# Layer 1's gates and memory queries by seven products of halves, in a stage ahead of its heads

## The chip, the core and the metric

The kernel runs on one core of a Trainium2 chip. The core has five engines, each with an instruction queue of its own that is worked off in order: TensorE (PE in the profile; its weight loads are PEld), VectorE (DVE), ScalarE (ACT), GpSimd (POOL), and SyncE (SP), which here only issues DMAs. They wait for one another through semaphores. Matmul operands lie in SBUF (128 partitions), matmul results in PSUM, which has eight banks of 128 x 512 fp32.

The metric is the device time of one execution in microseconds. Three runs of the kernel before gave 1555.32, 1557.88 and 1558.98 us, median 1557.88.

## The reference

A two-layer encoder over 1024 tokens of width 1024. Each layer normalises its input, makes one large input projection that feeds several groups of attention heads and a gate, multiplies the heads' outputs by silu of the gate, and projects back with a residual. Layer 0 has global heads, window heads and four memory heads; layer 1, which the change is about, has 16 heads of neighbourhood attention (C) and four memory heads:

```python
h = rmsnorm(x, norm_gain[l])
...
qc, kc, vc, qm, gate = split_cols(h @ w_in_odd[o], SPLIT_ODD)
yc = neighborhood_attn(qc.reshape(B, S, C_HEADS, HEAD_DIM),
                       kc.reshape(B, S, C_HEADS, HEAD_DIM),
                       vc.reshape(B, S, C_HEADS, HEAD_DIM), rpb_c[o])
ym = memory_attn(qm.reshape(B, S, M_HEADS, M_HEAD_DIM), mk, mv)
y = jnp.concatenate([yc, ym], axis=-1) * jax.nn.silu(gate)
x = x + y @ w_out_odd[o]
```

In layer 1, `qc`, `kc` and `vc` have 1024 columns each, `qm` 512 and `gate` 1536.

## The kernel before

Tokens lie along the free dimension (columns) and features along the partitions, so a normalised input is eight tiles of 128 features x 1024 tokens. All matmuls are fp32r, and a product keeps fp32 precision by three of them: every operand is split into a high part (a copy rounded to fp32r, made by ACT or POOL) and a low part (the difference, made by DVE or POOL), and high x high, high x low and low x high are summed in PSUM. The normalised input is held as tiles `H`, eight high ones and eight low ones. In the code `self.split`, `self.w_parts` and `self.wparts` are such splits; a weight block is loaded as `wraw`, and its parts are `wh` and `wl`, of four buffers each.

A projection of 128 columns (`tokens`, `token_steps`) takes two halves of 512 tokens, each 8 feature tiles x 3 matmuls of 128x512: 48 matmuls in a bank `pj`. A sink (`q_pair`, `k_pair`, `gate`, `mem_q`) then takes the result out of PSUM.

A scheduler puts the instructions of each engine in an order before the run; the program's own order is the start, `self.ahead(kind)` moves a group ahead or back by a number of the table `AHEAD`, `issue_after` ties a group behind one instruction, and `keep_in_program_order` pins one. Work can be put off: `put_off` and `lazily` collect generators in `self.waiting`, and `pull(n)` issues the next n steps of them.

The program's stages are: preparation, layer 0's heads (phase `l0`), its output projection (`out_project`), layer 1 (phase `l1`, function `odd`), and its output projection.

`out_project` already works by seven products: the weights and the gated outputs are cut into halves, sums of halves of the weights are made beforehand by POOL (`weight_sums`), and of the outputs when they are gated. It ends with the second half of the tokens (columns 512 to 1023): for each of its eight tiles the residual is added, `square` makes a square on ACT (tile `bt`, one buffer) and POOL adds the squares up (`vt`); the last addition, on DVE, gives the row sums of squares `rows1`. The first half's statistics come earlier, and that half is normalised completely (`norm_split`). For the second half, `each` puts the tokens times the gain, without their norm, into `H` (`with_gain`), and layer 1 multiplies by the norm later: `with_rstd` multiplies a sink's input by the norm along the columns (DVE, tile `vt`) where the column is from `raw_from` on, and `values` and `mem_att` use the norms as a scale per row.

Layer 1 begins with the first two memory queries, and after the first half of the first one `stats` computes the norms: four small matmuls (`rstd_cols`), eleven small DVE operations for the reciprocal root (`rq_v`, `rq_i`, `rq_y`, `rq_t`), and four transposes that turn them into rows (`rows_of`). Then come four memory heads (`mem_att`), with the values' projections (`values`), the other memory queries and a gate for each head issued between them in whole, and eight pairs of neighbourhood heads (`near_head`). A neighbourhood head has eight blocks of 128 queries: scores (two matmuls, tile `s`), bias and maximum (DVE, tile `pn`), exponential (ACT), reciprocal (DVE), normalisation (POOL), transposes on PE (`tr`), high and low parts (`ph` by ACT, `pl` by DVE), and the products with the values (`pv`). Behind each pair stand its gate (48 matmuls), `gated_rows` and the next pair's keys and queries (96 matmuls); the scheduler spreads them over the heads. The last pair has other cover: two gates put off and the begin of the output projection.

## Time and profile before

| what | us |
|---|---|
| median of three runs | 1557.88 |
| the profiled execution, its own time | 1557.26 |
| its span, first to last instruction | 1555.4 |
| busy in the span: PE, DVE, ACT, POOL | 1507.2, 993.5, 789.2, 742.8 |
| output projection of layer 0 ends, layer 1's projections begin | at 812 |
| layer 1's memory heads | about 842 to 1040 |
| layer 1's neighbourhood heads | about 1045 to 1414 |

The profile is that of one execution. Its page gives busy time and shares for each engine and the chain of work that ended last; the answers of the trace used below list groups of instructions (line of the code, engine, operation, output<-inputs, shapes, count, busy time in us, mean in ns, and the engine's idle time ahead of them with what ended it), waits, stretches, and single instructions in order of time. A matmul's listed duration runs from its own start, while its predecessor may still be draining, so durations of matmuls overlap.

### The profile page before, as it was taken

To read this page: it belongs to the slowest core of one execution; us is meant where nothing else is said; L and a number is where in the kernel's file an instruction comes from. 1 tells how busy PE (TensorE), PEld (TensorE's weight loads), DVE (VectorE), ACT (ScalarE), POOL (GpSimd) and SP (SyncE) were. 2 spreads that over 40 slices of the span, in tenths; PEclk is the share of its full clock that TensorE was granted. 3 is DMA by queue.
4 is the path that set the end of the run, shared out by engine and by line. 5 is a ranking of instruction groups with operands and counts; after the bars stand their busy time and mean duration, and the time that the engine had idled before them with its cause. 6 is when DMAs were issued, how large, how long until landed. Compare 5 with 4: busy or idle time off the path is not lost.

```text
span 1555.4 us, 24589 instructions
## 1 busy us (share of the span) xinstructions
PE 1507.2 (97%) x8166; PEld 1290.7 (83%) x8166; DVE 993.5 (64%) x2162; ACT 789.2 (51%) x1798; POOL 742.8 (48%) x859
## 2 busy tenths in 40 slices
PE   6999999999999999999999999999999999989997
PEld 5899898888888788778877878888888888878786
DVE  7768677767676668777483242346666666676654
ACT  8644556656655355655352232335554555565443
POOL 2513455546474545533464151246554666654454
PEclk7999999999999999999999999999999999999998
DMA  9535333132231513278545243444354554657844
GB/s 350 184 98 160 96 101 117 62 137 89 82 126 51 169 39 109 95 237 296 174 143 163 82 135 109 151 117 129 128 159 130 168 176 148 189 164 263 287 124 134
DMA packets 156670, 228.32 MB, mean 147 GB/s; under 512 B 13184, under 2 KB 95360, under 8 KB 155520
## 3 DMA queue, kind: packets, MB, share of 16 engines
q1 hardware_dynamic: 155680, 226.02, 44.9%
q8 instruction: 64, 1.05, 0.3%
q10 hardware_dynamic: 864, 0.74, 0.2%
q14 instruction: 62, 0.51, 0.1%
HBM read 152.26 MB, written 65.01 MB: 140 GB/s over the span
## 4 chain that ended last, share of the span: by engine, by line
PE 83%; DMA 5%; DVE 5%; ACT 3%; POOL 2%; issue 2%; SPq 0%; DVEq 0%; ACTq 0%; POOLq 0%
PE pj L212 34%; PE tr L107 9%; PE pj L363 6%; PE pv L907 4%; PE sa L1102 3%; PE pj L1102 3%; PE pv L944 3%; PE pj L704 3%; PE tr L1102 2%; PE sa L874 2%; PE sa L875 2%; PE s L1102 2%; PE pj L145 1%; DMA wraw<-w_o 1%; PE s L961 1%
## 5 line engine op out<-in xcount | busy, mean ns | idle before, releaser
L212 PE MATMUL pj<-H,wh 128*128 128x512 f32 x1696 | 559.4, 405 | 1.3 <-DVE q L301 0.7
L212 PEld LDWEIGHTS pj<-H,wh 128*128 128x128 f32 x1696 | 304.9, 189 | 53.2 <-DVE q L301 1.0
L212 PE MATMUL pj<-H,wl 128*128 128x512 f32 x848 | 336.5, 397 | 0.0
L99 ACT ACTIVATE ph<-tr 128x512 fp32r<-128x512 f32 (+2 forms) x336 | 178.9, 540 | 182.8 <-PE tr L107 179.2
L428 DVE TENSOR_TENSOR pl<-tr,ph 128x512 fp32r<-128x512 f32 (+2 forms) x336 | 204.6, 615 | 62.8 <-ACT ph L99 60.3
L212 PEld LDWEIGHTS pj<-H,wl 128*128 128x128 f32 x848 | 160.0, 189 | 34.6
L129 POOL TENSOR_SCALAR wh<-wraw 128x512 fp32r<-128x512 f32 x114 | 74.2, 651 | 192.3 <-PE pj L212 163.4
L130 POOL TENSOR_TENSOR wl<-wraw,wh 128x512 fp32r<-128x512 f32 x114 | 153.9, 1352 | 23.5 <-ACT wh L99 13.4
L107 PE MATMUL tr<-ident,P 128*128 128x128 f32 x816 | 127.4, 275 | 2.5 <-POOL P L585 2.0
L1056 POOL TENSOR_TENSOR wl<-wraw,wh 128x384 fp32r<-128x384 f32 x56 | 63.2, 1130 | 111.1 <-ACT wh L99 93.2
L975 POOL TENSOR_SCALAR pn<-pn,st 128x384 f32<-128x384 f32 (+1 forms) x128 | 75.6, 594 | 79.8 <-DVE st L974 66.6
L99 ACT ACTIVATE wh<-wraw 128x384 fp32r<-128x384 f32 (+1 forms) x138 | 73.4, 540 | 76.3 <-PE tr L1102 14.7
L107 PEld LDWEIGHTS tr<-ident,P 128*128 128x128 f32 x816 | 97.7, 141 | 12.8 <-POOL P L585 3.0
L882 POOL TENSOR_SCALAR P<-P,st 128x1024 f32<-128x1024 f32 x64 | 75.5, 1182 | 67.0 <-DVE st L881 61.2
L973 ACT ACTIVATE pn<-pn,st 128x384 f32<-128x384 f32 (+1 forms) x128 | 74.7, 585 | 40.7 <-DVE st L972 36.8
L880 ACT ACTIVATE P<-sa,st 128x1024 f32<-128x1024 f32 x64 | 71.5, 1118 | 41.6 <-DVE st L879 22.3
L518 POOL TENSOR_SCALAR P<-P,st 128x256 f32<-128x256 f32 x64 | 31.6, 510 | 124.9 <-DVE st L516 124.8
L879 DVE TENSOR_REDUCE st<-sa 128x1 f32<-128x1024 f32 x64 | 77.6, 1218 | 13.0 <-PE sa L875 12.0
L363 PE MATMUL pj<-k,H 128*128 128x512 f32 x256 | 81.4, 390 | 0.0
L969 DVE CUSTOM_DVE_ANT_0 pn<-s,bm 128x384 f32<-128x384 f32 x96 | 52.5, 555 | 35.6 <-PE s L962 15.6
L704 PE MATMUL pj<-ah,H 128*128 128x256 f32 x384 | 73.3, 287 | 0.0
L585 POOL TENSOR_SCALAR P<-P,st 128x384 f32<-128x384 f32 (+1 forms) x64 | 39.1, 628 | 59.3 <-DVE st L580 51.7
(416 smaller groups left out, 3586.3 us busy)
## 6 DMA issues: line engine op xcount, KB each, us to landing
wraw<-w_o SPq DMA_DIRECT2D x80, 256.0 KB, 3.0
y<-sg SPq DMA_DIRECT2D x24, 512.0 KB, 2.9
y<-yb SPq DMA_DIRECT2D x24, 512.0 KB, 3.1
wraw<-s SPq DMA_DIRECT2D x64, 192.0 KB, 3.6
wraw<-w_e SPq DMA_DIRECT2D x44, 256.0 KB, 3.0
k<-k SPq DMA_DIRECT2D x36, 256.0 KB, 4.5
wraw<-w_mem SPq DMA_DIRECT2D x32, 256.0 KB, 4.4
v<-ph SPq DMA_DIRECT2D x32, 256.0 KB, 2.1
```

Of the source, the lines that this page charges most:

```text
L99: return self.nc.scalar.activation(out, in_, AF.Copy, scale=scale)
L107: self.turned = self.fence = self.nc.tensor.transpose(o, i, self.ident)
L130: (nc.gpsimd if self.wsplit[1] == "pool" else nc.vector).tensor_tensor(lf, raw, hf, op=OP.subtract)
L212: last = nc.tensor.matmul(a[:, :n], s[:, kt % UNIT, :], m, start=(kt == 0 and i == 0), stop=(kt == KT - 1 and i == 2))
L363: nc.tensor.matmul(p, x[kt][:, t], m, start=(kt + i == 0), stop=(kt == KT - 1 and i == 2))
L428: nc.vector.tensor_tensor(pl[:, :n], tr[:, :n], ph[:, :n], op=OP.subtract)
L704: self.last = nc.tensor.matmul(a[:, b * 256:(b + 1) * 256], x[kt][:, t], w, start=(kt + b + i == 0), stop=(kt == KT - 1 and i == 2), skip_ ...
L879: nc.vector.tensor_reduce(st[:, 0:1], s, axis=AX.X, op=OP.max, negate=True)
L882: self.normal = nc.gpsimd.tensor_scalar(pt, pt, st[:, 2:3], 0.5, op0=OP.mult, op1=OP.mult)
L973: nc.scalar.activation(o, o, AF.Exp, bias=st[:, 1:2], accum_out=st[:, 2:3])
L975: normal = nc.gpsimd.tensor_scalar(o, o, st[:, 3:4], 0.5, op0=OP.mult, op1=OP.mult)
L1102: last = nc.tensor.matmul(bank, s[:, k, :], y[3 * u + k][m][:, cols], start=start and u + k + e == 0, stop=u == 1 and k + e == 4, skip_gro ...
```

## The change

A new stage, `front`, stands between layer 0's output projection and layer 1's heads. It computes ten of layer 1's twelve gates (8 to 11 and 0 to 5) and its four memory queries, in seven pairs of projections. With the weights of a pair cut into quarters (two column blocks by two halves of the features) and the tokens into quarters (two halves of the features by two halves of the tokens), a pair is a product of 2x2 by 2x2 blocks, and it is made by seven block products in place of eight. A block product is 12 matmuls of 128x512.

The seven products need sums and differences of the quarters. On the weights' side they are four operations of 128x512 for each pair (`sums`, on POOL; on DVE for the second pair). On the tokens' side they are made once (`operands`): the second half is now normalised completely, in `x1`, the fp32 tiles that the output projection left (tags `P` and `yb`, in a pool `mid` that lives on into the stage); from it and the first half the differences t1 to t4 are made and split into parts. The differences of t1 and t2 are DVE's, those of t3 and t4 POOL's; all low parts of t1 to t4 are DVE's. `each`, `with_gain`'s use for the second half, and the multiplication by the norm in layer 1's sinks fall away (`raw` takes the place of `raw_from`, and only layer 0 has it).

While these operands are made, PE works on the two products of the first five pairs that need only the first half of the tokens (`begin` and `second`, 24 matmuls a pair): 24 of those ahead of the statistics, 12 between them and the turn into rows, and 60 behind the turn, ahead of the first product with t1; the remaining 24 stand between the first pair's products with t1 and t2. `begin` uses five banks `x`, `second` the one bank `pv`, which DVE must have read before it is used again.

Results go to DRAM: a gate as gate x (1 + tanh) (512 tokens a store), a memory query as high and low parts. Layer 1 loads them with one DMA a tile.

In layer 1 the values' projections are put off and pulled in steps of 12 matmuls at the memory heads, and the keys and queries of the next pair are put off and pulled in steps of 3 matmuls, two steps a block. The copies of a key's halves to the other partitions move into its sink.

In the diff, the first part is the new stage:

```diff
+    def front(self, w, pairs, early, order, x1, squares, dests):
...
+        def operands():
+            with self.ahead("norm"):
+                y = self.rstd_cols([squares], 1, 4)
+            yield self.last
+            with self.ahead("norm"):
+                rows = self.rows_of(y, 4)
...
+                for n in range(len(todo) + 2):
+                    if n < len(todo):
+                        x, kt, _, _ = todo[n]
+                        d = nc.vector.scalar_tensor_tensor(x, x, self.gain[:, 8 + kt:9 + kt], rows, op0=OP.mult,
+                                                           op1=OP.mult)
+                        if n:
+                            pin(d)
+                    low = late.popleft() if n > 1 else None
+                    if 0 < n <= len(todo):
+                        x, kt, dst, t = todo[n - 1]
+                        d, f = minus(dst, x, dst, t, v)
+                        pin(d)
+                        late.append(f)
+                    if low:
+                        pin(low())
+                for k in range(4):
+                    to_h(b22[k], 4 + k)
+                for dst, a, b, ts in ((b22, b22, b12, t3), (b21, b11, b21, t4)):
+                    for k in range(4):
+                        d, f = minus(dst[k], a[k], b[k], ts[k], g)
+                        pin(d)
+                        f()
...
+        def begin(j):
+            xs.append(self.ps("x"))
+            ws = unit(self.wload(w[pairs[j][0]][:, 0:512]), g)
+            with tc.issue_after(fence.ins) if fence else nullcontext():
+                product(xs[j], ws, of_h(0, 0))
...
+        def sums(a11, a12, a21, a22, engine=g):
...
+                for o, a, b, op in ((s1, a21, a22, OP.add), (a21, a11, a21, OP.subtract), (a11, s1, a11, OP.subtract),
+                                    (a12, a12, a11, OP.subtract)):
...
+            product(y, unit(s1, e), t1)
...
+            product(x, unit(a11, e), t2, False)
...
+            product(x, unit(a21, e), t3, False)
...
+            product(y, unit(a12, e), of_h(1, 1), False)
...
+            product(z, unit(a22, e), t4)
```

The second part is what changes around it and in layer 1:

```diff
-                def each(nt, x):
-                    self.with_gain(x, 8 + nt, self.h[0][nt][:, 512:], self.h[1][nt][:, 512:])
...
+                pairs = [(O_G + g, O_G + g + 1) for g in (8, 10, 0, 2, 4)] + [(O_QM, O_QM + 1), (O_QM + 2, O_QM + 3)]
+                self.front(wo, pairs, 5, (0, 1, 2, 5, 6, 3, 4), x1, rows1, dests)
...
+        self.waiting += [self.values(w[O_V:], vd, g) for g in range(2)]
...
+        q0 = self.q_pair(w, O_Q)
+        self.pull(1)
...
-            if h in (0, 2):
-                self.values(w[O_V:], vd, h // 2)
...
-            self.gated_rows(self.gate(w, O_G + 8 + h), 8 + h, y, yd)
+            self.gated_rows(gate(8 + h), 8 + h, y, yd)
...
-            if j == 7:
+            if j < 7:
+                with self.put_off():
+                    now = qkv(j + 1)
...
-                self.near_head(q[i], ks[i], v, i, bm[i], y, side)
+                self.near_head(q[i], ks[i], v, i, bm[i], y, side, 2 if j < 7 else 3)
```

What the scheduler makes of it is shown at three places. The first is DVE where the norms of layer 1's second half have just been computed. Before, the last steps of the root were followed by the sink of a memory query (`q`) and by the values' parts (`ph`), operations with one operand in PSUM (`pj`):

```order
L234 SCALAR_TENSOR_TENSOR rq_y_9334<-rq_t_9335,rq_y_9334 128x4
L1300 TENSOR_SCALAR rs_147<-rq_y_9334 128x4
L1301 TENSOR_SCALAR rm_148<-rq_y_9334 128x4
L103 TENSOR_TENSOR q_9383<-pj_9396,q_9382 128x512
L103 TENSOR_TENSOR q_9383<-pj_9423,q_9382 128x512
L370 TENSOR_TENSOR ph_9513<-pj_9488,ph_9513 128x4x64
```

Now the normalisation (L1243, `tr` is the turned norms in PSUM), the differences (L1226), the lower parts of t1 (L1228) and the end of a gate (L1297, L1283) follow:

```order
L234 SCALAR_TENSOR_TENSOR rq_y_9372<-rq_t_9373,rq_y_9372 128x4
L1243 SCALAR_TENSOR_TENSOR P_8124<-P_8124,gain_65,tr_9404 128x512 x2
L1226 TENSOR_TENSOR P_8128<-P_8124,P_8128 128x512
L1243 SCALAR_TENSOR_TENSOR P_8125<-P_8125,gain_65,tr_9404 128x512
L1226 TENSOR_TENSOR P_8128<-P_8124,P_8128 128x512
L1297 TENSOR_TENSOR vt_9492<-vt_9492,pv_9473 128x512
L1228 TENSOR_TENSOR t_1926_9295<-P_8128,t_1925_9294 128x512
L1243 SCALAR_TENSOR_TENSOR P_8125<-P_8125,gain_65,tr_9404 128x512
L1226 TENSOR_TENSOR P_8129<-P_8125,P_8129 128x512
L1283 SCALAR_TENSOR_TENSOR vt_9492<-vt_9495,vt_9492 128x512
```

From the turn to the last lower part of t4, DVE has 50 operations of 128x512 now: 12 with an operand in PSUM (8 of L1243, 4 of L1297) and 38 with both tiles in SBUF.

The second place is POOL over the same stretch. Before, the additions of squares (L1118) and weight parts stood there, and then four low parts of the values' weights:

```order
L1118 TENSOR_TENSOR vt_8933<-vt_8933,bt_9189 128x512
L129 TENSOR_SCALAR wh_9392<-wraw_9390 128x512
L130 TENSOR_TENSOR wl_9387<-wraw_9384,wh_9386 128x512
L130 TENSOR_TENSOR wl_9393<-wraw_9390,wh_9392 128x512
L1118 TENSOR_TENSOR vt_8933<-vt_8933,bt_9225 128x512
L357 TENSOR_TENSOR v_9454<-wraw_9460,k_9450 128x512
```

Now, behind the last addition of squares, a weight part and four sums of weight quarters (`wq`), these rows lead up to the last difference of t4 (L1054 weight parts, L1233 lower parts of tokens, L1226 differences):

```order
L1054 TENSOR_TENSOR wl_9530<-wraw_9527,wh_9529 128x512
L1054 TENSOR_TENSOR wl_9556<-wraw_9553,wh_9555 128x512
L1054 TENSOR_TENSOR wl_9575<-wraw_9572,wh_9574 128x512
L1233 TENSOR_TENSOR H_8870<-yb_8130,H_8862 128x512
L1054 TENSOR_TENSOR wl_9601<-wraw_9598,wh_9600 128x512
L1054 TENSOR_TENSOR wl_9627<-wraw_9624,wh_9626 128x512
L1233 TENSOR_TENSOR H_8871<-yb_8130,H_8863 128x512
L1233 TENSOR_TENSOR H_8872<-yb_8131,H_8864 128x512
L1233 TENSOR_TENSOR H_8873<-yb_8131,H_8865 128x512
L1226 TENSOR_TENSOR yb_8130<-yb_8130,P_8124 128x512 x2
L1226 TENSOR_TENSOR yb_8131<-yb_8131,P_8125 128x512 x2
L1226 TENSOR_TENSOR P_8126<-P_8128,P_8126 128x512 x2
```

With two more differences that makes 17 operations, where there were four.

The third place is PE in the neighbourhood heads. Before, projection matmuls (`pj`) stood in pieces of any length between transposes (`tr`), scores (`s`) and value products (`pv`):

```order
L107 MATMUL tr_11767<-ident_63,pn_11757 128x128
L944 MATMUL pv_11703<-pl_11729,v_11542 128x256
L212 MATMUL pj_12101<-H_8869,wh_12070 128x512
L212 MATMUL pj_12101<-H_8861,wl_12071 128x512
L212 MATMUL pj_12101<-H_8862,wh_12070 128x512
L944 MATMUL pv_11703<-ph_11748,v_11542 128x384
L961 MATMUL s_11844<-k_11548,q_11628 128x256
```

Now every block has the same form: three transposes, two steps of three projection matmuls, the low product of the block before, two scores, the high product of this block:

```order
L110 MATMUL tr_13023<-ident_63,pn_13016 128x128
L215 MATMUL pj_12999<-H_8860,wh_12875 128x512
L215 MATMUL pj_12999<-H_8868,wh_12875 128x512
L215 MATMUL pj_12999<-H_8860,wl_12876 128x512
L215 MATMUL pj_12999<-H_8861,wh_12875 128x512
L215 MATMUL pj_12999<-H_8869,wh_12875 128x512
L215 MATMUL pj_12999<-H_8861,wl_12876 128x512
L942 MATMUL pv_12844<-pl_12964,v_12309 128x256
L959 MATMUL s_13173<-k_12317,q_12320 128x384
L960 MATMUL s_13173<-k_12318,q_12320 128x384
L942 MATMUL pv_12845<-pl_12964,v_12309 128x128
L942 MATMUL pv_12844<-ph_12995,v_12309 128x128
```

Over the whole program PE has 8056 matmuls in place of 8140; the rest of its instructions are as they were, apart from their order in layer 1.

## What was predicted

> **What bounds the kernel now.** I read the busy shares of the page first, then its chain of work, then the stretches that the change touches.
>
> ```profile
> PE 1507.2 (97%) x8166; PEld 1290.7 (83%) x8166; DVE 993.5 (64%) x2162; ACT 789.2 (51%) x1798; POOL 742.8 (48%) x859
> PE 83%; DMA 5%; DVE 5%; ACT 3%; POOL 2%; issue 2%; SPq 0%; DVEq 0%; ACTq 0%; POOLq 0%
> ```
>
> TensorE (PE) is busy for 97% of the span and carries 83% of the chain. A share over the whole span mixes stages, so the next table gives the stages: first the neighbourhood heads of layer 1, then its memory heads, then, for comparison, the window heads of layer 0. Columns are the stretch, its length, and the busy time of PE, PE's weight loads, VectorE (DVE), ScalarE (ACT) and GpSimd (POOL) with their instruction counts, then clock and DMA.
>
> ```profile
> 1060.00:1340.00 280.00, 280.00 (x1501) 242.09 (x1500) 183.67 (x567) 147.55 (x361) 164.60 (x219) 1.00 0.49 150
> 842.00:1040.00 198.00, 196.67 (x935) 163.15 (x934) 66.17 (x129) 61.53 (x150) 53.31 (x67) 1.00 0.36 119
> 600.00:680.00 80.00, 74.68 (x417) 63.47 (x415) 63.94 (x167) 49.19 (x130) 34.99 (x47) 0.98 0.36 123
> ```
>
> In layer 1 PE never stands still for long, so a matmul taken away there is time, as long as the order that remains leaves no gap. The clock is full, so nothing is to be had from it.
>
> **What the change removes: 84 matmuls.** Seven pairs of 128-column projections (ten gates, four memory queries) cost 96 matmuls of 128x512 each now; by seven products of 12 they cost 84. The saving is 7 x 12 = 84. What one costs is read from a stretch that holds projection matmuls alone:
>
> ```profile
> 812.10:823.10 11.00, 10.97 (x48) 8.83 (x47) 1.00 0.51 165
> ```
>
> 48 in 10.97 us is 0.2285 us each, so **19.2 us** go from PE. (The group of these matmuls has a mean of 405 ns, since each is counted from its own start while the one ahead still drains; 84 of those would be 34 us. The Trainium skill, "Trainium Kernel Development and Optimization", section "Performance Expectations", says that matmul busy time is a poor measure because matmuls are pipelined; the spacing above agrees with it, and I use the spacing.)
>
> Three waits of PE stand at the same place of the program now:
>
> ```profile
> PE pj L1102 <- DVE wl L1056: 1.7, 1, 1.7
> PE tr L107 <- DVE rq_y L234: 1.3, 1, 1.3
> PE sa L1102 <- DVE wl L1056: 1.0, 1, 1.0
> ```
>
> The 1.3 us is the wait for layer 1's statistics, which moves into the new stage and is counted there: -1.3. The other two stand in the output projection, behind DVE's work for `each`, which is removed. I take half of 2.7, **-1.4** (bounds 0 and -2.7).
>
> **What it adds: a start that PE cannot cover.** The products t1 to t4 need the second half of the tokens normalised, which needs its row sums, the statistics, a turn on PE, and then a long pipeline on DVE, ACT and POOL. How late the row sums are now:
>
> ```profile
> 813.56 0.67 DVE L1111 TENSOR_TENSOR yb<-yb,tr 128x512 f32<-128x512 f32 x1
> ...
> 821.47 0.63 ACT L1116 ACTIVATE bt<-yb 128x512 f32<-128x512 f32 x1 [3.73 <-POOL vt L1118]
> 822.13 0.60 ACT L99 ACTIVATE q<-pj 128x512 fp32r<-128x512 f32 x1
> 822.14 0.69 DVE L1275 TENSOR_TENSOR rows<-vt,bt 128x512 f32<-128x512 f32 x1 [6.21 <-ACT bt L1116]
> ```
>
> The last residual is added at 813.6, and the row sums start at 822.1: the squares have one buffer (bt), and each waits for POOL's addition of the one before, which stands between weight parts on POOL. Now 48 matmuls (11 us) lie over that; in the new order 24 do (5.5 us).
>
> The decisive point is how DVE and POOL get on with each other:
>
> ```profile
> 807.79 1.30 POOL L1118 TENSOR_TENSOR vt<-vt,bt 128x512 f32<-128x512 f32 x1
> 807.96 0.72 ACT L99 ACTIVATE H<-yb,gain 128x512 fp32r<-128x512 f32 x1
> 807.98 1.67 DVE L648 SCALAR_TENSOR_TENSOR H<-P,gain,H 128x512 fp32r<-128x512 f32 x1
> 809.04 1.76 POOL L130 TENSOR_TENSOR wl<-wraw,wh 128x512 fp32r<-128x512 f32 x1
> 809.13 0.64 ACT L1116 ACTIVATE bt<-yb 128x512 f32<-128x512 f32 x1 [0.44 <-POOL vt L1118]
> 809.57 1.78 DVE L648 SCALAR_TENSOR_TENSOR H<-yb,gain,H 128x512 fp32r<-128x512 f32 x1
> ```
>
> ```profile
> 794.21 4.03 DVE L269 SCALAR_TENSOR_TENSOR P<-P,gain,tr 128x512 f32<-128x512 f32 x6
> ...
> 796.81 2.55 POOL L271 TENSOR_TENSOR H<-P,H 128x512 fp32r<-128x512 f32 x2
> ```
>
> ```profile
> 717.73 2.00 DVE L103 TENSOR_TENSOR H<-H 128x512 fp32r<-128x512 f32 x3
> ```
>
> In the first fence the two engines take turns. DVE's operation on two SBUF tiles begins at 807.98 and ends at 809.65, about 0.6 us after POOL's ended (809.09); POOL's next then ends at 810.80, about 1.2 us after DVE's; and so on. Alone the DVE one costs 0.65 us (2.00 for three) and the POOL one 1.27 (2.55 for two). The six DVE operations from 794.21 on, whose second tile is in PSUM, ran at 0.67 each while POOL was busy. So operations of DVE on two SBUF tiles and POOL's operations add up, and those with a PSUM operand lie beside them. (The Trainium skill, "SBUF — State Buffer", section "Who interferes with whom", states this as a lock on a shared pair of ports, held for the whole instruction, against a DVE instruction with two SBUF inputs while a GpSimd one reads SBUF. It speaks against this change, and the trace agrees: 1.67 us for 0.65.)
>
> Now the count, from the order of the changed kernel. Between the end of the output projection and the last lower part of t4, POOL has the last two additions of squares and two weight parts with them, 4 sums of weight quarters and 17 further operations (5 weight parts, 4 lower parts of tokens, 8 differences): 25 x 1.27 = 31.8 us. DVE has 38 operations on two SBUF tiles after the turn (8 differences, 16 lower parts of t1 to t4, 6 weight parts, 4 weight sums, 4 gate ends), 38 x 0.65 = 24.7, and ahead of it the row sums (0.7) and the root:
>
> ```profile
> 784.92 0.15 DVE L259 TENSOR_SCALAR rq_v<-pv 128x4 f32<-128x4 f32 x1
> ...
> 786.36 1.34 POOL L1118 TENSOR_TENSOR vt<-vt,bt 128x512 f32<-128x512 f32 x1 [2.97 <-ACT bt L1116]
> 786.46 1.26 DVE L230 TENSOR_SCALAR rq_y<-rq_i 128x4 int32<-128x4 int32 x1
> ...
> 790.50 0.16 DVE L234 SCALAR_TENSOR_TENSOR rq_y<-rq_t,rq_y 128x4 f32<-128x4 f32 x1
> ```
>
> A step of the root is 0.15 to 0.17 us alone and 1.26 under a POOL operation; the eleven steps are some 2.2 us of their own. In all 31.8 + 24.7 + 0.7 + 2.2 = **59.4 us** that cannot overlap, and about 3 us in which neither runs, while the squares, the turn on PE and the first normalised blocks pass: 62.4.
>
> PE has, in its order up to the end of the first t4 product, 182 matmuls of 0.2285 (41.6) and 1.4 us for the statistics and the turn: 43.0. The end of that product follows the last t4 part by 0.7. PE therefore stands still for 62.4 + 0.7 - 43.0 = **20 us** in all, first for the row sums and the root, then at t1, t2 and t4. The lower bound is 14 (no dead time, and the additions done early, as DVE is relieved); the upper is 29: if every wait in the queues counts (ACT's copies stand in order behind weight copies that wait for DMAs). Queued behind a waiting DVE operation are the gate ends, which free the one `pv` bank, so the filler products stop too.
>
> **The smaller parts.** The second pair needs a weight part that stands on POOL behind six weight sums and token parts, with a load ahead of them that waits for the first pair's last weight part: **+1.5** (0 to 4). From the third pair on, a pair costs PE 13.7 us or more (60 matmuls), POOL about 7 x 1.27 and DVE about 6 x 0.65 = 12.8 in sum: hidden. The gates' stores and loads are hidden by the same products.
>
> The memory heads lose their gates as cover and keep the values' 384 matmuls:
>
> ```profile
> L496 PE MATMUL s<-mk,q 128*128 128x256 f32 x32 | 9.2, 287 | 0.8 <-ACT P L512 0.8
> L107 PE MATMUL tr<-ident,P 128*128 128x128 f32 x64 | 10.5, 276 | 0.5 <-POOL P L518 0.5
> ```
>
> They wait for 1.3 us now, with more cover; I add **+1.5** (0 to 6), mostly for the first head, whose queries, keys and weights are loaded behind the last gates' stores on the SP queue.
>
> In the neighbourhood heads the gate matmuls go and the rest is spread evenly, six to a block:
>
> ```profile
> L212 PE MATMUL pj<-H,wh 128*128 128x512 f32 x548 | 178.1, 394 | 0.0
> L212 PE MATMUL pj<-H,wl 128*128 128x512 f32 x273 | 107.9, 395 | 0.0
> ```
>
> ```profile
> L969 DVE CUSTOM_DVE_ANT_0 pn<-s,bm 128x384 f32<-128x384 f32 x68 | 37.4, 555 | 25.2 <-PE s L962 10.7 <-PE tr L107 9.2 <-POOL pn L975 4.2
> L287 DVE TENSOR_TENSOR vt<-pj,rows 128x512 f32<-128x512 f32 x17 | 11.7, 689 | 13.9 <-PE pj L212 13.8
> L969 DVE CUSTOM_DVE_ANT_1 pn<-s,bm 128x256 f32<-128x256 f32 x24 | 10.1, 419 | 3.9 <-PE s L962 2.3 <-PE tr L107 1.3
> L387 DVE SCALAR_TENSOR_TENSOR sg<-sg,vt 128x512 f32<-128x512 f32 x6 | 4.6, 773 | 0.2 <-ACT sg L386 0.2
> L387 DVE SCALAR_TENSOR_TENSOR sg<-sg,pj 128x512 f32<-128x512 f32 x5 | 3.4, 685 | 2.0 <-ACT sg L386 2.0
> ```
>
> The stretch of 280 us holds 68 + 24 = 92 blocks and 821 projection matmuls, a third of them gates: 274 x 0.2285 = 62.6. Without them a block takes PE (280 - 62.6) / 92 = 2.36 us. DVE's 183.7 us lose 11.7 + 4.6 + 3.4 and become 164, 1.78 a block: 75% instead of 66%. The window heads, at 63.94 of 80 (80%), leave PE 5.3 us idle in 80, which is 6.6%. The scores are issued four blocks ahead, so I put the loss nearer to nothing: **+3** of 7 x 16 x 2.36 = 264 us (0 to 17).
>
> **Sum.** -19.2 - 1.3 - 1.4 + 20 + 1.5 + 1.5 + 3 = +4.1 us. The profiled execution took 1557.26 (its span of 1555.4 and 1.9 around it), 0.6 below the median of the runs, so the forecast is 1557.9 + 4.1 = **1562**.
>
> **Rivals.**
>
> *Faster: the start is bound by DVE alone.* If the turns seen above are rarer than my count has them, because POOL finds its operands late and works while DVE is on PSUM operands, then DVE's 50 operations after the turn are 38 x 0.65 + 12 x 0.67 = 32.7 us, against 30.6 of PE's until the first t4 product. PE loses 3 there and 2 ahead of the turn instead of 20: 1562 - 15 = **1547**. For it: DVE's order interleaves PSUM operations, and 120 matmuls have been put over the start. Against it: POOL's 17 operations must all be done before the last t4 part, and the rows above show strict turns. It decides at about 16 us of idle PE: less, and the change gains.
>
> *Slower still: the heads run out of cover.* With 6.6% of 264 us, as in the window heads, the neighbourhood heads lose 17 us instead of 3: **1576**. The place is the blocks at a pair's end, where DVE's product of gate and output on 1024 columns (two SBUF tiles) can sit under a POOL operation while transposes wait. For it: DVE at 75% with one block between a transpose and its use; against it: PE lost nothing at 66%. It decides from about 70% DVE upwards, if PE's waits grow as between those two stages.
>
> **How the numbers follow.** My forecast has 0.54, the faster rival 0.32, the slower one 0.14. What a measurement of this kernel can tell from no change is about 0.2%, or 3.1 us (1554.8 to 1561.0). The forecast's own range, with 14 to 29 us at the start and the small terms in their bounds, is 1552 to 1573; of its 0.54, 0.06 lie below 1554.8, 0.16 within, 0.32 above. The faster rival gives 0.31 faster and 0.01 same. So faster 0.37, same 0.17, slower 0.46. The range of 8 in 10 reaches to both rivals: 1544 to 1579.
>
> **What would show it.** Right: between the last output product and the first t4 product PE is idle for some 20 us in the profile after, with waits put down to DVE's t1, t2 and t4 parts and the root, DVE and POOL in turn, and DVE's two-SBUF operations near 1.9 us from start to start. Wrong at that step: idle under 12 us there, with DVE operations of 0.65 beside busy POOL. The 84 matmuls are right if PE's count falls by 84 and its spacing stays 0.2285. The heads are right if a block takes 2.36 us and PE is idle for less than 2% there; above 5% the slower rival holds. Memory heads that idle for over 6 us would be a cause that I priced too low.

## The result, and the profile after

The changed kernel takes 1577.3 us (median of 4 runs, 1573.5 to 1580.0) against 1557.5 (1555.3 to 1559.0) of the kernel before: a ratio of 1.0127, 95% interval 1.0102 to 1.0151. So the change costs 19.8 us, where I had forecast 4.1. The profiled execution of the changed kernel was its longest, 1580.0; in the profiles the difference is 1578.2 - 1555.4 = 22.8 us, and the sums below are made against that.

The page's busy line and its chain by engine, which answer to the first two lines of the prediction:

```profile
PE 1502.0 (95%) x8082; PEld 1279.5 (81%) x8082; DVE 1049.4 (66%) x2210; ACT 838.6 (53%) x1890; POOL 779.8 (49%) x870
PE 37%; DMA 3%; DVE 1%; issue 1%; POOL 1%; ACT 1%; SPq 0%; DVEq 0%; POOLq 0%; ACTq 0%
```

This chain is followed back only as far as 888 us: its shares add up to 44% of the span. So PE's 37% of the span, out of 44, can't be set beside the 83% of the chain before.

PE's count fell by 84, as the change says, but its busy time by 5.2 us and not by 19.2, and its idle time rose from 48.2 to 76.2. Where, is read from the windows by stage. First the changed kernel: the new stage, the memory heads up to the first score of the neighbourhood heads, the neighbourhood heads up to their last product with the values (which stands among the first products of the output projection), the final projection. (Columns: stretch, length, PE busy, weight loads, DVE, ACT, POOL, clock, DMA share and GB/s.)

```profile
811.17:975.10 163.93, 143.80 (x602) 114.29 (x601) 105.03 (x123) 71.45 (x126) 104.08 (x73) 0.95 0.34 120
975.10:1128.23 153.13, 146.46 (x705) 119.05 (x703) 61.98 (x125) 58.28 (x152) 43.03 (x56) 1.00 0.62 206
1128.23:1459.70 331.47, 321.72 (x1754) 277.87 (x1755) 237.35 (x763) 206.14 (x502) 194.20 (x270) 0.99 0.63 196
1459.70:1578.20 118.50, 105.40 (x491) 87.04 (x489) 65.71 (x110) 47.93 (x92) 54.96 (x50) 0.95 0.53 175
```

The kernel before, with the same borders, has no new stage:

```profile
812.13:1044.78 232.65, 230.04 (x1086) 190.41 (x1085) 79.85 (x156) 72.22 (x168) 77.65 (x89) 1.00 0.39 127
1044.78:1436.82 392.04, 387.78 (x2058) 333.26 (x2057) 263.01 (x799) 210.05 (x514) 225.89 (x297) 1.00 0.52 164
1436.82:1555.40 118.58, 106.05 (x490) 85.85 (x489) 64.66 (x111) 49.99 (x94) 55.66 (x50) 0.95 0.56 183
```

The order of the two programs gives the matmuls of 128x512 that each stage lost or got; at 0.2285 us each they say how long a stage would be if nothing else had changed. What is left over is the loss:

| stage | without loss | after | loss | forecast |
|---|---|---|---|---|
| layer 0, to the last output product | 812.1 | 811.2 | -1.0 | -1.4 |
| new stage: 588 matmuls and 1.4 for statistics and turn | 135.8 | 163.9 | **+28.2** | +21.5 |
| to the neighbourhood heads: 384 fewer, 15 more, and without the 2.7 us of statistics and the wait for them | 145.6 | 153.1 | **+7.5** | +1.5 |
| neighbourhood heads: 303 fewer | 322.8 | 331.5 | **+8.7** | +3.0 |
| final projection | 118.6 | 118.5 | -0.1 | 0 |

With -19.2 for the matmuls and -1.3 for the old wait that makes +22.8. Three places each lost some 6 us more than I had put down.

In the new stage, PE's waits up to the first t4 product are these (engine, waiting operation, what it waited for: total, times, longest):

```profile
PE x L1274 <- DVE t L1228: 7.5, 2, 5.8
PE pv L1274 <- DVE vt L1297: 4.5, 2, 2.8
PE y L1274 <- DVE wl L1054: 3.3, 1, 3.3
PE pv L256 <- DVE rows L1465: 2.8, 1, 2.8
PE tr L110 <- DVE rq_y L234: 0.9, 1, 0.9
PE x L1274 <- DVE wl L1054: 0.6, 1, 0.6
```

All six name DVE: 19.6 us idle, where 20 were forecast. They do not all stand where they were forecast: 7.5 us are at t2, 2.8 and 0.9 at the row sums and the root, 8.4 at the `pv` bank and at lower weight parts, and none at the parts of t1 and t4. What comes on top is seen in PE's own rows behind the longest wait (start, length, operation; the wait ahead in brackets) and in the clock of 4 us stretches:

```profile
861.05 0.79 PE L1274 MATMUL x<-t,wh 128*128 128x512 f32 x1 [5.81 <-DVE t L1228]
861.65 0.63 PE L1274 MATMUL x<-t,wl 128*128 128x512 f32 x1
862.07 0.63 PE L1274 MATMUL x<-t,wh 128*128 128x512 f32 x1
864.40 0.79 PE L1274 MATMUL x<-t,wh 128*128 128x512 f32 x1 [1.70 <-DVE t L1228]
...
868.30 0.63 PE L1274 MATMUL pv<-H,wl 128*128 128x512 f32 x1
868.73 0.63 PE L1274 MATMUL pv<-H,wh 128*128 128x512 f32 x1
```

```profile
860.00:864.00 4.00, 1.65 (x3) 0.83 (x3) 4.00 (x3) 0.99 (x2) 4.00 (x4) 0.50 0.17 66
864.00:868.00 4.00, 1.94 (x4) 1.12 (x5) 4.00 (x6) 1.89 (x4) 1.48 (x1) 0.50 0.01 2
868.00:872.00 4.00, 4.00 (x11) 3.13 (x10) 3.44 (x6) 1.41 (x3) 0.00 (x0) 0.50 0.48 156
```

From 861 to about 872 the clock is 0.50, and a matmul takes 0.42 to 0.43 us from start to start (861.65 to 862.07, 868.30 to 868.73). Summed over 4 us stretches (busy time times what the clock lacks to 1), the slow clock takes 5.6 us of PE's time in this stage. That is not what the stage would be shorter by at full clock, since part of the slow matmuls stand ahead of a further wait for DVE. The other 3.0 of the 28.2 are 0.5 us of later waits and, by elimination, 2.5 us for the ends of the matmuls ahead of each wait, which count as busy.

### The profile page after: what moved, and what is told of

It reads as the page before. It is cut to its first block, busy times and chain, and to the rows that moved or that the text cites. A ratio compares the mean times of both kernels' runs of the same rounds, so it can differ in the third digit from the quotient of the medians.

```text
span 1578.2 us, 24720 instructions
## 1 busy us (share of the span) xinstructions
PE 1502.0 (95%) x8082; PEld 1279.5 (81%) x8082; DVE 1049.4 (66%) x2210; ACT 838.6 (53%) x1890; POOL 779.8 (49%) x870
## 5 line engine op out<-in xcount | busy, mean ns | idle before, releaser
L215 PE MATMUL pj<-H,wh 128*128 128x512 f32 x1248 | 418.4, 416 | 0.6 <-DVE vt L286 0.4
L215 PE MATMUL pj<-H,wl 128*128 128x512 f32 x624 | 247.9, 397 | 0.0
L215 PEld LDWEIGHTS pj<-H,wh 128*128 128x128 f32 x1248 | 215.0, 191 | 32.9 <-PE sa L560 0.8
L215 PEld LDWEIGHTS pj<-H,wl 128*128 128x128 f32 x624 | 118.0, 189 | 28.4
L1054 POOL TENSOR_TENSOR wl<-wraw,wh 128x384 fp32r<-128x384 f32 (+1 forms) x69 | 81.4, 1182 | 118.8 <-ACT wh L102 104.0
L102 ACT ACTIVATE wh<-wraw 128x384 fp32r<-128x384 f32 (+1 forms) x155 | 84.0, 549 | 92.0 <-PE tr L1100 17.3
L133 POOL TENSOR_TENSOR wl<-wraw,wh 128x512 fp32r<-128x512 f32 x86 | 112.1, 1306 | 22.0 <-ACT wh L102 14.5
L973 POOL TENSOR_SCALAR pn<-pn,st 128x384 f32<-128x384 f32 (+1 forms) x128 | 76.8, 602 | 90.8 <-DVE st L972 53.4
L110 PE MATMUL tr<-ident,P 128*128 128x128 f32 x752 | 117.5, 275 | 1.9 <-POOL P L583 1.8
L132 POOL TENSOR_SCALAR wh<-wraw 128x512 fp32r<-128x512 f32 x86 | 56.4, 656 | 123.5 <-PE pj L215 92.8
L971 ACT ACTIVATE pn<-pn,st 128x384 f32<-128x384 f32 (+1 forms) x128 | 74.8, 585 | 36.2 <-DVE st L970 30.5
L110 PE MATMUL tr<-ident,pn 128*128 128x128 f32 x352 | 66.9, 275 | 4.9 <-POOL pn L973 4.4
L583 POOL TENSOR_SCALAR P<-P,st 128x384 f32<-128x384 f32 (+1 forms) x64 | 38.9, 625 | 59.9 <-DVE st L578 54.6
```

The lines of the kernel that those rows point to most:

```text
L102: return self.nc.scalar.activation(out, in_, AF.Copy, scale=scale)
L110: self.turned = self.fence = self.nc.tensor.transpose(o, i, self.ident)
L133: (nc.gpsimd if self.wsplit[1] == "pool" else nc.vector).tensor_tensor(lf, raw, hf, op=OP.subtract)
L215: nc.tensor.matmul(a[:, :n], s[:, kt % UNIT, :], m, start=(kt == 0 and i == 0), stop=(kt == KT - 1 and i == 2))
L973: normal = nc.gpsimd.tensor_scalar(o, o, st[:, 3:4], 0.5, op0=OP.mult, op1=OP.mult)
L1054: engine.tensor_tensor(lf, raw, hf, op=OP.subtract)
```

## The experiments

Theory A: the start of the new stage waits for operands that DVE and POOL make, and the clock is slow behind the waits. Theory B: the heads, which lost their gates, are the main loss. All kernels are edits of the changed kernel; differences show its lines with - and +. The column "new stage" is the length from the first product of that stage to the end of its last, in the profile.

| label | us, median | ratio to before, 95% | new stage, us |
|---|---|---|---|
| (changed kernel) | 1577.3 | 1.0102 to 1.0151 | 163.9 |
| no_differences | 1561.5 | 1.0007 to 1.0033 | 148.5 |
| plain_ahead | 1573.8 | 1.0093 to 1.0126 | 160.6 |
| differences_on_vector | 1578.3 | 1.0113 to 1.0150 | 163.6 |
| gates_back_as_cover | 1641.4 | 1.0521 to 1.0560 | 163.7 |
| filler_matmuls | 1577.1 | 1.0108 to 1.0139 | 164.6 |
| squares_on_vector | 1572.9 | 1.0079 to 1.0109 | 160.6 |
| two_pairs_plain | 1568.5 | 1.0045 to 1.0078 | 162.0 |
| plain_normalised_first | 1568.6 | 1.0045 to 1.0082 | 157.1 |
| weights_first | 1569.8 | 1.0040 to 1.0078 | 157.1 |
| two_banks | 1567.2 | 1.0033 to 1.0074 | 157.7 |
| values_between_scores | 1580.7 | 1.0131 to 1.0161 | 164.0 |
| two_banks_values_late | 1580.2 | 1.0109 to 1.0153 | 159.0 |

Executions of one kernel lie up to 9 us apart, so a small step is read from the stage and not from the time. The stage repeats better: three profiles with the same program in it (the changed kernel, gates_back_as_cover, values_between_scores) give 163.7 to 164.0 us, two others (two_banks and two_banks_values_late) 157.7 and 159.0. There is one profile for each kernel, and the stages behind the new one differ more from profile to profile. The profile of the changed kernel is of its longest execution, those of plain_normalised_first and weights_first are of their fastest (1564.3 and 1563.6 us).

### What the differences cost, and what the place costs

```
-product(y, unit(s1, e), t1)
+product(y, unit(s1, e), of_h(0, 0))
...
-product(z, unit(a22, e), t4)
+product(z, unit(a22, e), of_h(1, 0))
```

(`minus` and its lower parts are gone from `operands`, and t2 and t3 are replaced in the same way.)

> The differences t1 to t4 are left out (their 16 subtractions, 16 copies and 16 lower parts); their products take the normalised blocks instead, so the gates and queries are not the reference's. Matmuls and weights are as in the changed kernel. Theory A (the start of the new stage waits for these operands, and the clock is slow behind the waits): of 27 us lost at the start, the waits for row sums and root (3.7 us and some 2 us of slow clock) stay, 21 go: 1577 - 21 = 1556 us, PE idle in the start 4 to 6 us instead of 19.7. Theory B (the start is a minor loss, the heads that lost their gates are the cause): 1571 to 1577 us.

In plain_ahead, `operands` normalises and splits the eight blocks only, and each block of a pair's outputs is computed by this:

```
+def whole(nt, c, ws):
+    p = self.ps("x")
+    product(p, ws[0], of_h(0, c))
+    product(p, ws[1], of_h(1, c), False)
...
```

> The same ten gates and four queries ahead of the heads, kept in DRAM, but each by twelve plain products of 128x512 per pair (96 matmuls a pair instead of 84) from normalised halves; no differences, no weight sums. Theory A: 84 matmuls more are +19.2 us, the stall at the differences goes (-21): 1575 us; so the place alone, without the seven products, costs 18 us against the kernel before, 5 of them at the start and 13 in the heads. Theory C (the heads cost no more than the 4.5 us net of my terms): 1567 us. Theory B (heads alone lose 35): 1592 to 1597 us.

Without the differences the same 588 matmuls take 15.5 us less, and the kernel 15.8: theory A's sign, and three quarters of the 21. What was not foreseen is a wait of 3.2 us at a lower weight part, whose DVE operation again took turns with POOL. Plain products need 153.6 us for 672 matmuls and 1.4 for the statistics, so this stage, 160.6 us long, loses 5.7 us. That splits the result: the seven products save 19.2 us and bring 28.2 - 5.7 = 22.5 of extra loss at the start, a net loss of 3.3 (3.5 by the times); the other 15.8 us (1573.8 against 1558.1 of before beside it) come with computing gates and queries ahead of the heads at all. By the marks set beforehand A stands in both runs (1556 and 1575 expected, 1561.5 and 1573.8 measured) and B falls (1571 to 1577, and 1592 to 1597), as does C (1567). But A's own sum for plain_ahead put 13 us into the heads, and they are there: its memory heads take 152.2 us and its neighbourhood heads 329.2, against the 145.6 and 322.8 of the table above, a loss of 6.6 and 6.4. So the start alone does not explain the result.

### Is it the turns, or DVE's queue?

```
-g.tensor_tensor(l, x, h, op=OP.subtract)
+(v if kt >= 4 else g).tensor_tensor(l, x, h, op=OP.subtract)
...
-d, f = minus(dst[k], a[k], b[k], ts[k], g)
+d, f = minus(dst[k], a[k], b[k], ts[k], v)
```

> The 8 differences of t3 and t4 and the 4 lower parts of b22 go from POOL to DVE (same work, other engine). Theory A with the two engines taking turns: each costs 1.25 us of the shared time on POOL and 0.60 on DVE, so 12 x 0.65 = 7.8 us less; the waits at t2 shrink by 5 to 8 us and some of the slow clock goes: 1570 us (1567 to 1573). Theory D (DVE's own queue is the bound, the turns cost nothing): 12 x 0.6 = 7 us more on DVE, 1577 to 1584 us.

A's gain did not come. The 1578.3 us and the stage of 163.6 lie at the lower end of what D expected, but D's reason, that the turns cost nothing, does not hold either. These rows of the changed kernel's timeline show the turns, POOL's first and then DVE's (POOL's eight differences need 13.5 us, and DVE's operations start every 1.7):

```profile
851.99 6.79 POOL L1226 TENSOR_TENSOR yb<-yb,P 128x512 f32<-128x512 f32 x4
858.74 6.74 POOL L1226 TENSOR_TENSOR P<-P,P 128x512 f32<-128x512 f32 x4
```

```profile
860.92 1.76 DVE L1228 TENSOR_TENSOR t<-yb,t 128x512 fp32r<-128x512 f32 x1
862.60 1.74 DVE L1228 TENSOR_TENSOR t<-P,t 128x512 fp32r<-128x512 f32 x1
```

In the experiment DVE works alone at this place and starts every 0.60 us, but then POOL's other work meets it:

```profile
854.16 0.67 DVE L1226 TENSOR_TENSOR yb<-yb,P 128x512 f32<-128x512 f32 x1
854.77 0.67 DVE L1336 TENSOR_TENSOR wq<-wq 128x512 f32<-128x512 f32 x1
...
870.58 1.75 DVE L1283 SCALAR_TENSOR_TENSOR vt<-vt,vt 128x512 f32<-128x512 f32 x1
872.25 1.78 DVE L1228 TENSOR_TENSOR t<-P,t 128x512 fp32r<-128x512 f32 x1
```

So the turns are real, but the edit did not take them away. In the changed kernel DVE does 50 operations from the turn (826.7) to the last lower part (874.3). 38 at 0.60 and 12 at 0.60 to 0.66 are 30.5 us; it was idle for 1.6; the other 15.6 of the 47.7 are turns. Counted in the same way, DVE in the experiment does 64 operations of 38.9 us in all from 827.1 to 880.5, is idle for 2.1, and the turns are still 12.5 of 53.4 us, since POOL's weight sums and token parts, which had stood behind, now meet the later part of DVE's queue. The edit added 8 us of operations to the queue and saved 3 of turns, so the last lower part came some 6 us later. The stage is no longer for it; in the changed kernel PE reached the t4 product 4.3 us after its operands were ready, which left room for most of that. What the start would cost without turns, no run here shows.

### Is the start a chain from the row sums?

```
-nc.gpsimd.tensor_tensor(sums[0], sums[0], sq, op=OP.add)
+(nc.gpsimd if last or k < 3 else nc.vector).tensor_tensor(sums[0], sums[0], sq, op=OP.add)
```

> The last four additions of squares in layer 0's output projection go from POOL, where they stand between weight parts, to DVE, which is idle there. The row sums come 2 to 3 us earlier, and the first wait of 2.8 us and the slow clock behind it (1.7 us) go. If the start is a chain that begins with the row sums, the new stage gets shorter by 2.5 to 4.5 us: 163.9 to about 160. Rival (the later waits take it back, since DVE and POOL are busy without a break from the turn on): 0 to 1 us.

1572.9 us, 4.4 less, and the stage 3.3 less: as theory A had it. The wait for the row sums is gone from PE's rows.

### The slow clock

```
+for _ in range(fill[k]):
+    tc.keep_in_program_order(nc.tensor.matmul(d, ws[0][:, 0, :], of_h(0, 0)[0][0], start=True, stop=True, ...))
...
-product(x, unit(a11, e), t2, False)
+product(x, unit(a11, e), t2, False, (0, 0, 20, 6) if j == 0 else None)
```

> 26 matmuls of 128x512 whose result nobody reads go into TensorE's order right ahead of the two t2 products that waited 5.8 and 1.7 us (20 and 6); 26 x 0.2285 = 5.9 us of work in a 7.5 us wait. They add nothing to what the kernel computes. Theory F (the clock is slow in the 7 us behind a long idle time because of that idle time): the matmuls behind the wait run at 0.23 us instead of 0.43, and the start of the new stage, 163.9 us long in the changed kernel, is 2 to 4 us shorter. Rival (the clock is not ruled by the idle time): no shorter, or longer by up to 6 us.

```profile
854.45 4.74 PE L1276 MATMUL tr<-H,wh 128*128 128x512 f32 x20
859.03 0.40 PE L1279 MATMUL x<-t,wh 128*128 128x512 f32 x1
860.74 0.50 PE L1279 MATMUL x<-t,wh 128*128 128x512 f32 x1 [1.31 <-DVE t L1228]
861.07 0.40 PE L1279 MATMUL x<-t,wl 128*128 128x512 f32 x1
865.89 1.22 PE L1279 MATMUL pv<-H,wh 128*128 128x512 f32 x2 [4.42 <-DVE vt L1304]
```

The 20 matmuls fill the wait, and the next ones run at full speed (860.74 to 861.07 with the restart; 0.60 and 0.42 in the changed kernel). Then PE waits 4.4 us for the `pv` bank and the clock is slow again. The clock therefore follows the idle time, as theory F says; its gain does not come: the stage is 164.6 us long, because DVE frees the bank no earlier. The wait for it ended 56.15 us behind the stage's begin here (865.89 and 809.74) and 56.11 in the changed kernel (867.28 and 811.17). How much the slow clock alone costs can't be read from this run.

### Do the neighbourhood heads lack cover?

```
     now = qkv(j + 1)
+    if j < 6:
+        sgj = self.gate(w, O_G + j)
...
-self.gated_rows(gate(j), j, y, yd)
+self.gated_rows(sgj, j, y, yd)
```

> The new stage stays whole, and beside it the six gates of the neighbourhood heads are computed a second time inside them, 48 matmuls each, in the steps between blocks; the heads use these. 288 matmuls more are +65.8 us if no gap takes them up. Theory E (the heads lost some 9 us for want of cover: 10 us idle and slow clock behind it): +57, 1634 us, and PE idle between 1160 and the last pair falls from 1.4% to near nothing. Rival: the heads' loss is not one of cover: 1641 to 1643 us.

1641.4, which is 64.1 us more: in the rival's range. PE's idle share in the middle of the heads did fall as E has it, from 1.4% (197.12 us busy of 200) to 0.2%:

```profile
1160.00:1360.00 200.00, 199.65 (x1069) 172.03 (x1068) 124.51 (x393) 104.15 (x257) 113.31 (x159) 1.00 0.51 153
```

These are the waits in the neighbourhood heads, first of the changed kernel, then of the experiment:

```profile
PE tr L110 <- POOL pn L973: 4.4, 1, 4.4
PE s L959 <- DVE st L967: 3.8, 7, 0.7
PE s L960 <- DMA k<-k: 0.7, 1, 0.7
PE s L959 <- DMA k<-k: 0.3, 1, 0.3
```

```profile
PE pv L942 <- ACT ph L102: 2.5, 1, 2.5
PE tr L110 <- POOL pn L973: 1.8, 3, 1.3
PE s L960 <- DMA k<-k: 0.7, 1, 0.7
PE s L959 <- DVE st L967: 0.3, 1, 0.3
```

By stages, the experiment's heads take 393.9 us, with 15 matmuls fewer than in the kernel before (392.0): a loss of 393.9 - 392.0 + 15 x 0.2285 = 5.3 instead of 8.7. This step of 3.4 us is within the scatter of the stage: eleven other profiles with the same program in it give 326.8 to 332.8 us, where the changed kernel's has 331.5. What the cover surely takes back are the seven waits of the scores, one in each of seven pairs: 3.8 us in the changed kernel, 3.6 to 3.8 in those eleven, 0.3 with the gates. That is less than half of E's 9 us. What stays are the keys' copies by DMA (1.0) and waits in the last pair with slow clock behind them; their cause no run here settles.

### Cover for the start

```
+for j in range(2):
+    ws = raw(j)
+    n1, n2 = pairs[j]
+    u = unit(ws[2]), unit(ws[3])
+    whole(self.ps("x"), n2, 0, u)
+    whole(self.ps("y"), n2, 1, u)
+    whole(self.ps("pv"), n1, 1, (unit(ws[0]), unit(ws[1])))
```

> The first two pairs take twelve plain products each, the other five seven; so 24 matmuls of 12 x 2 more than in the changed kernel (+5.5 us), and the first four of the plain products (48 matmuls, 11 us) need no normalised second half, the next 96 only the normalised one and no differences. 8 weight sums fall away. If the loss at the start is lack of work for TensorE while DVE and POOL prepare t1 to t4, its 28 us fall to about 6 (the wait for row sums and its slow clock): the stage takes 163.9 - 28 + 6 + 5.5 = 147 us (145 to 151), the kernel 1577 - 16 = 1561. Rival (other waits, weights or banks, hold the start): above 157 us.

(The edit also splits the first four normalised blocks earlier, and puts pair 3 ahead of the memory queries.)

The stage took 162.0 and not 147, so the rival held. The time fell by 8.8 us, in the profiles by 9.2, of which the stage shows 1.9: 2.7 lie ahead of it and 3.2 in the final projection, where the program is the same. PE waits no longer for a difference, but 2.8 us for the row sums, and longest of the rest at a weight part and at the `pv` bank:

```profile
840.07 1.00 PE L1274 MATMUL x<-H,wh 128*128 128x512 f32 x2 [4.88 <-ACT wh L102]
863.25 0.73 PE L1274 MATMUL pv<-H,wh 128*128 128x512 f32 x2 [2.22 <-DVE vt L1297]
```

Three steps followed, the first on top of two_pairs_plain and each of the other two on top of that first one. In the first the squares go to DVE as above, and all blocks are normalised ahead of the differences:

```
+for n, (x, kt, _, _) in enumerate(todo):
+    d = nc.vector.scalar_tensor_tensor(x, x, self.gain[:, 8 + kt:9 + kt], rows, op0=OP.mult, op1=OP.mult)
...
+    to_h(x, kt)
+for x, kt, dst, t in todo:
+    d, f = minus(dst, x, dst, t, v)
...
```

> Two pairs by plain products as before in two_pairs_plain, the squares' last additions on DVE, and in the operands' order all eight blocks of the second half are normalised first, with their copies, and the differences only behind them. In two_pairs_plain ScalarE's copies of weights stood behind copies of blocks that DVE had not yet normalised, since its differences and lower parts stood between; TensorE waited 4.9 us for one. If this order is the cause, that wait goes and with it part of the slow clock, and the row sums' wait of 2.8 us goes as well: the stage takes 161.9 - 4.9 - 2.8 - 3 = 151 us (147 to 155) and the kernel 1558 to 1562. Rival (DVE and POOL are busy without a break whatever their order, and the waits for the one pv bank and for weights return): 158 us or more, 1565 or more.

The stage fell to 157.1, between the two, and 3.3 us of the 4.9 are what the squares alone had given; by the time (1568.6, the same as two_pairs_plain) the rival holds. The weight's wait is 1.9 instead of 4.9, but the bank's waits are 8.4:

```profile
PE pv L1267 <- DVE vt L1290: 8.4, 2, 5.0
PE x L1267 <- ACT wh L102: 1.9, 1, 1.9
```

In the second the weight parts went first (`w=100` became `w=400` in the table of priorities):

> plain_normalised_first with the weight parts of the new stage ahead of the operands in the queues of ScalarE, DVE and POOL. If what is left of the start's loss is weight parts queued behind operands, the stage gets shorter by 2 to 6 us against plain_normalised_first. Rival: the operands then come later and the products of the other five pairs wait for them by as much: within 1 us, or longer.

No change: 157.1 and 1569.8. The third gives the early products two banks in turn:

```
-z = self.ps("pv")
+z = self.ps(("pv", "y")[j % 2])
```

> plain_normalised_first with the second halves of the five early products put by turns into the banks pv and y instead of pv alone. What was left there is 1.9 us at a weight part, 5.0 and 3.5 us at the one pv bank, which DVE frees late, and 4.3 us of slow clock behind them; no wait for a difference. If the bank is the cause, 6 to 8 us of waits and 2 to 4 us of slow clock go: the stage takes 146 to 149 us instead of 157.1, and the kernel 1558 to 1561, level with the kernel before. Rival (DVE's queue gives the bank's successor or the differences just as late): 154 us or more.

No change either, 157.7 and 1567.2. The waits moved to the two banks' turn:

```profile
845.15 0.73 PE L1267 MATMUL pv<-H,wh 128*128 128x512 f32 x2 [3.84 <-DVE vt L1290]
856.76 1.22 PE L1267 MATMUL y<-H,wh 128*128 128x512 f32 x2 [4.70 <-DVE vt L1290]
```

A bank comes free when DVE reaches its addition in its queue, and that queue has no gap from 821 to 861. More banks or another order only change which wait names DVE. No version here beats the kernel before.

### Where the values' steps stand in the memory heads

The edit is `self.pulls = (2, 0)` instead of `(1, 1)`; the last run has `(0, 2)` on top of two_banks.

> In layer 1's memory heads the steps of the values' projection are issued two after each pair of score blocks and none behind the transposes (now one and one). The heads lost 6.3 us there, with 2.6 us of waits of the scores for the exponentials and 1.9 of the transposes for the normalised weights. If it is the place of the cover, these two waits go and others of 1 to 2 us come at the products behind the transposes: the stretch of 153.2 us gets 2 to 4 us shorter. Rival (the work on the other engines ahead of each step sets it): no change or longer.

> two_banks with the steps of the values' projection in layer 1's memory heads two behind the transposes and none between score blocks (the other way round cost 3 us more in that stretch). If the transposes' side is short of cover, the stretch of 152 us gets 2 to 3 us shorter, the kernel 1555 to 1558; if both places need theirs, it gets 2 to 4 us longer.

The stretch took 156.6 us instead of 153.1, and 159.4 instead of 155.3 in two_banks: 3.5 and 4.1 longer. Eleven profiles with one step at each place give 151.5 to 155.3, so the first lies 1.3 us beyond that scatter and the second 4.1. The times are 1580.7 and 1580.2. The second is 13 us above two_banks, in the profiles 14.2: 4.1 in this stretch, 4.6 ahead of the new stage, 1.2 in it, 0.3 at the end, and 4.0 in the neighbourhood heads, whose first scores waited 5.9 us for the keys' copies instead of 0.9. As far as the two runs go, both places need their step. What is missing against the kernel before are the gates that stood beside them. The waits of the changed kernel in this stretch:

```profile
PE s L494 <- ACT k L509: 2.6, 2, 1.6
PE tr L110 <- POOL k L515: 1.9, 3, 0.9
PE pj L365 <- POOL v L358: 1.5, 2, 0.9
```

That their lack is the cause is argued from the two runs; a run that puts matmuls back there was not made.

## Why the prediction was right or wrong

**The 84 matmuls: right.** The count fell by 84; 413 matmuls in 94.5 us of busy time, at full clock, is 0.229 us each in the stage's undisturbed part:

```profile
880.00:975.00 95.00, 94.54 (x413) 77.25 (x412) 48.42 (x55) 40.20 (x71) 56.73 (x42) 1.00 0.40 139
```

**The chain of DVE and POOL: right in mechanism; that its size fits is in part luck.** I counted 62.4 us from the last output product to the last t4 part, which puts it at 811.2 + 62.4 = 873.6; it ended at 874.3. The engines took turns at 1.7 us. But two errors of the count cancel in the main: the 12 operations on PSUM, put at nothing beside POOL's, took 7.7 us of DVE's queue, and POOL's 17 operations there, put at 17 x 1.27 = 21.6 us, cost it 15.6 us of turns. PE stood still for 19.6 us, of 20; this too fits by more than the mechanism, since 8.4 us of it are waits at the bank and at weight parts, and the sum that gave 20 ends at a wait that PE did not have, as follows.

**The step that failed there is "The end of that product follows the last t4 part by 0.7".** The first t4 product started at 878.65 without a wait, 4.3 us after its last operand, and ended at 881.4, 7 us behind that part. PE's last wait had not been for t4 but for the `pv` bank, and it ended at 867.28, with 50 matmuls still to come up to the end of the t4 product, which PE ran without a gap:

```profile
867.28:881.40 14.12, 14.12 (x50) 11.39 (x51) 10.07 (x15) 7.60 (x15) 6.42 (x5) 0.80 0.33 112
```

At 0.2285 us they are 11.4 us. So of the lateness 2.7 us are the slow clock behind that wait (0.80 in the mean), and the larger part is work: at full clock the product would have ended at 878.7, still 4.4 us behind the part. I had read "the clock is full, so nothing is to be had from it" from the stretch before and carried it into a stage with waits of 3 to 6 us, where it is not; and I had taken the last operand for PE's last wait. This lateness is nearly the whole of 28.2 against 21.5 (bounds 14 to 29 and 0 to 4). The slow matmuls at 821 to 825 and at 861 to 865 stood ahead of further waits, so they probably took the place of idle time; what the stage would take at full clock, no run shows. The second pair cost 0.5, of 1.5.

**The faster rival fell.** Its count for DVE alone held: 32.7 us, against 30.5 of operations and 1.6 of idle time. But DVE was bound by more than itself: 15.6 us of turns stand on top.

**The memory heads: mis-sized.** I put +1.5 (0 to 6); they lost 7.5, with PE idle for 6.7 us (6 to 10 over the eleven profiles named above). That is the case named as "a cause that I priced too low". I had kept the values as cover and priced only the first head, but the waits stand in several heads, at scores, transposes and values alike.

**The neighbourhood heads: mis-sized, within the bounds.** +3 (0 to 17) became +8.7, or 4 to 10 over the profiles with the same program in this stage. Slow clock takes 3.1 us in the changed kernel's stage, in the first and the last pair, against 1.7 in the kernel before. In the middle they are as forecast: 83 blocks in 200 us is 2.41 us a block, of 2.36, and 1.4% idle:

```profile
1160.00:1360.00 200.00, 197.12 (x1105) 171.86 (x1104) 147.05 (x484) 128.13 (x314) 129.95 (x182) 1.00 0.62 193
```

The loss that I missed stands at the borders: a score's wait in each of seven pairs, the first pair's keys, the last pair. Over the whole stage 2.9% is idle, between my two marks of 2% and 5%; the slower rival's place (the product of gate and output at a pair's end) is not among the waits, though its total of 1576 is close to what was measured.

**The output projection** gave 1.0 us, of 1.4.

So the sign was right, and the sum was short by 6.7 us at the start, 6.0 in the memory heads and 5.7 in the neighbourhood heads. The 1577.3 us lie in the range of 8 in 10 (1544 to 1579), but above the forecast's own range of 1552 to 1573. That range was not the sum of its terms' bounds: with every term at its bound the sum goes from 1549 to 1593, and to 1579 with the neighbourhood heads left at +3. That the result still lies within the wide range, which was drawn up to the slower rival, whose place did not show, is in part luck.

## What to carry to other kernels

When matmuls are taken out of a stage where they covered other engines, price the place that loses them, border by border, before counting the saving: here the move alone cost 15.8 us, most of what a saving of 19.2 could have paid. The start of the new stage took its operands, in the main, from one engine's queue, DVE's. Another engine, order or bank for part of that work moved the wait (differences_on_vector, weights_first, two_banks: no gain), and only work taken off the queue (no_differences) or an earlier start of it (squares_on_vector) shortened the stage. When a chain of operands is counted against TensorE's work, look for the last operand that it really waits for and add what stands behind it: here 50 matmuls. And a wait of the size seen here, 2.8 to 5.8 us, had slow matmuls behind it in most cases here; they add to the time where no further wait follows.

## What the hardware showed that I had not expected

The granted clock falls to 0.50 behind a wait, for up to 11 us when more waits follow. It is not decided by the length of the wait alone. PE's wait of 2.84 us up to 840.45 in the changed kernel left the matmuls behind it at 0.23 us; the same wait of 2.82 us in filler_matmuls left them at half speed:

```profile
840.00:844.00 4.00, 3.50 (x14) 1.00 0.01 4
```

```profile
840.00:844.00 4.00, 4.00 (x13) 0.67 0.00 0
```

(Windows of PE alone, the changed kernel's first: length, busy, clock, DMA.) The Trainium skill, "TensorE: Matmul & The Clock Gate", section "Part 1: The HAM clock gate (the "warmup" mystery)", says that a monitor halves TensorE's clock after an idle window of about 3.4 us and that the window runs freely, so that the moment of a change varies with where in it the matmuls fall. Two like waits with unlike ends agree with a window that runs freely. The half clock behind a wait of 2.82 us does not agree with 3.4 us of idle time, and here the measurement decides. The 0.43 us of a slow matmul agree with the Trainium skill, "TensorE: Matmul & The Clock Gate", section "Wait — 56ns, not 53.3ns?", which gives 426.7 ns for 512 columns.

Slow stretches also come and go where the program is the same: the neighbourhood heads took 326.8 us in filler_matmuls, without one, and 331.5 in the changed kernel, with 3.1 us of slow clock in two places. This may be part of why executions of one kernel lie several us apart; no run here shows it for one and the same kernel.
